# Layer 0's down projection by Strassen's scheme, in a two-layer decoder kernel

## The chip, the cores and the metric

The kernel runs on one core of a Trainium2 chip. The metric is the device time of one execution in microseconds (us). Engines are called PE (TensorE, matmuls), DVE (VectorE), ACT (ScalarE), POOL (GpSimd) and SP (SyncE, which issues most DMAs).

## The reference

Two layers on 512 tokens of width 1024, all in fp32. Layer 0 is a Mamba-2 mixer and a ConvFFN; then keys and values are projected from the normed stream; layer 1 is differential attention and a ConvFFN. The change lies in layer 0's ConvFFN, in its last matrix product:

```python
def conv_ffn(x, ln_g, up_w, conv_w, conv_b, down_w):
    u = causal_dwconv(rms_norm(x, ln_g) @ up_w, conv_w, conv_b)
    gate, up = u[..., :FFN_DIM], u[..., FFN_DIM:]
    return (jax.nn.silu(gate) * up) @ down_w          # FFN_DIM = 2816

def shared_kv(x, kv_ln_g, kv_w, k_norm_g):            # on the stream behind layer 0
    kv = rms_norm(x, kv_ln_g) @ kv_w
    ...
```

## The kernel before, in words

The stream is held transposed, as `xT`: eight blocks of 128 features by 512 tokens. Each fp32 value is split into a high half that fits PE's fast fp32 form and the rest, so a product takes three matmuls: high by high, high by low, low by high (`mm3`, L208 to L210). For the stream the halves are `xgh` (ACT, L483) and `xgl` (DVE, L484).

Weights come in chunks of at most 128x1024, in the order of a list, `plan`. For each chunk SP loads the raw tile `wr`, ACT copies the high half `wh` (L148, `high`), DVE subtracts for the low half `wl` (L159, `low`). Taking a chunk emits the work on the chunks up to two places ahead of it (`chunk`, `emit_chunk`). The chunks for keys and queries are scaled by a gain as they are split (L173 on ACT, L174 on DVE). PSUM has two rings of four banks, `mm` and `aux`.

A ConvFFN is the function `ffn`. Its 22 hidden blocks of 128 features run in parts: gate and up products of a part first ("g" and "u" chunks), then the part's share of the down projection. A gate or up product has 24 matmuls of 512 columns; its taps are an addition-like step on DVE (L957), one on ACT (L958) and two of 511 or 510 elements on DVE (L960); then come SiLU (ACT, L1127) and the product of both (DVE).

Layer 0 has two parts, of 12 and 10 blocks. Each hidden block is split into `hh` (L1140, ACT) and `hl` (L1141, DVE), 512 tokens wide. The down projection takes four groups of 256 features (two banks `ps_d` each); weights are stationary, tokens move, 512 columns a matmul. After each group `add_to_stream` adds both banks to `xT` (L571). In the last part it also makes `xgh` and `xgl` for the next projection, squares the block (L557, ACT) and adds the square to the norm's sum `nacc` (L559, on POOL, for the last block on DVE).

Layer 1 already uses Strassen's scheme (`down_tokens`) in parts of 8, 8 and 6 blocks. There a pair of hidden blocks (even and odd) and two token halves give four quarters; `operands` builds four sums of them (L1035) and splits them (`sh` L1038 ACT, `sl` L1039 DVE). The weights' sums are made by accumulating DMAs that POOL issues into the tiles `wz` (`plus`, L986) or by DVE; `combine` splits them (L1008, L1009). The seven products are named "1" to "7", in the order 1257634; a running sum of some of them collects what several outputs share (L1059). In layer 1 the token operands are stationary and 512 weight columns move.

Behind layer 0's FFN the first projection is `k0` (function `proj`), whose chunks of two feature blocks are read in the order 0, 2, 4, 6. The Tile framework's scheduler orders each engine's queue; waits between engines are semaphores. PE's queue is written by hand in attention alone.

Of the kernel before, what the change touches and what calls it, by code (L numbers as in the profile page):

```python
# [18 lines left out]
P = 128  # L19
T = 512  # L20
# [12 lines left out]
SEVEN = "1257634"  # L33
# [8 lines left out]
def trunk_kernel(ctx: ExitStack, tc, x, ssm_ln_g, ssm_in_w, ssm_conv_w, ssm_conv_b, ssm_dt_bias,  # L42
# [48 lines left out]
    def ffn_plan(l):  # L91
        for p0, p1 in PARTS_D if l else ((0, HALF), (HALF, NPAIR)):
            for p in range(p0, p1):
                plan.append(("g%d_%d" % (l, p), *w_cols(ffn_up_w[l], 0, KB, p * P, P)))
                plan.append(("u%d_%d" % (l, p), *w_cols(ffn_up_w[l], 0, KB, FFN + p * P, P)))
            if l == 1:
                for m in SEVEN:
                    for q0 in range(0, (p1 - p0) // 2, 2):
                        plan.append(("s%s_%d_%d" % (m, p0, q0), (m, p0, q0, min(2, (p1 - p0) // 2 - q0))))
                continue  # L100
            for c in range(4):
                for k in range(p0, p1, 4):
                    plan.append(("d%d_%d_%d" % (l, c, k),
                                 *w_cols(ffn_down_w[l], k, min(4, p1 - k), c * 256, 256)))

    ffn_plan(0)

    def tok_plan(key, w, c0, gcol):
        for k in range(0, KB, 2):
            plan.append(("%s_%d" % (key, k), *w_cols(w, k, 2, c0, 512), gcol + k))  # L110
# [78 lines left out]
    def emit_chunk():  # L189
        i = state["next"]  # L190
        if i < len(plan):
            state["next"] = i + 1
            if len(plan[i]) == 2:
                state["combine"](plan[i][0], *plan[i][1])
# [39 lines left out]
    xgh = [gp.tile([P, T], F32R, name="xgh%d" % k) for k in range(KB)]  # L234
    xgl = [gp.tile([P, T], F32R, name="xgl%d" % k) for k in range(KB)]
# [265 lines left out]

    def token_rsqrt(acc, pl, name, n):
# [42 lines left out]
    class Norm:  # L545
# [6 lines left out]
        def add(self, k):  # L552
# [6 lines left out]
            (dve if k == KB - 1 else pool).tensor_tensor(out=self.acc, in0=self.acc, in1=sq, op=ALU.add)  # L559

# [373 lines left out]
    def ffn(l, norm, bp, gnext, nnext):  # L934
        with tc.tile_pool(name="ffn_h%d" % l, bufs=1) as hp, tc.tile_pool(name="ffn%d" % l, bufs=1) as fp:
# [13 lines left out]
            def taps(j, p, ps):  # L949
# [4 lines left out]
                v = fp.tile([P, T], F32, tag="v%d" % j, name="v" + key, bufs=3 if j or nnext is not None else 4)  # L954
# [21 lines left out]
            raws = {}  # L976

            def source(p0, q0, nq, j, i):
                src = ffn_down_w[l][(p0 + 2 * q0) * P:(p0 + 2 * q0 + 2 * nq) * P, i * 512:(i + 1) * 512]
                return src.rearrange("(k j p) c -> j p k c", j=2, p=P)[j]  # L980

            def view(t, nq):
                return t[:, :nq * 512].rearrange("p (k c) -> p k c", k=nq)

            def plus(t, p0, q0, nq, j, i):
                pool.dma_start(view(t, nq), source(p0, q0, nq, j, i), accum_op=ALU.add)  # L986

            def ahead(p0, n, behind):

                for k, j, i in ("z", 0, 0), ("x", 0, 1), ("y", 1, 1):  # L990
                    for q0 in range(0, n // 2, 2):
                        c, nq = q0 // 2, min(2, n // 2 - q0)
                        pool.tensor_copy(raws[k][c][:, 0:1], behind[:, 0:1])
                        sync.dma_start(view(raws[k][c], nq), source(p0, q0, nq, j, i))

            def combine(key, m, p0, q0, nq):

                c, n = q0 // 2, nq * 512
                if m == "2":
                    t = wrp.tile([P, 1024], F32, tag="raw", name="wr_" + key)  # L1000
                    sync.dma_start(view(t, nq), source(p0, q0, nq, 1, 0))
                else:
                    t = raws["x" if m == "7" else "y" if m == "3" else "z"][c]
                    if m == "7":
                        dve.tensor_tensor(out=t[:, :n], in0=t[:, :n], in1=raws["y"][c][:, :n], op=ALU.add)
# [5 lines left out]
                if m in "156":  # L1011
                    plus(t, p0, q0, nq, *{"1": (0, 1), "5": (1, 1), "6": (1, 0)}[m])

            if nnext is None:
                raws["z"] = [fp.tile([P, 1024], F32, name="wz%d" % c) for c in range(2)]
# [3 lines left out]
                state["combine"] = combine  # L1019
                run_sum = fp.tile([P, 2, T], F32, name="run_sum")  # L1020

            def operands(p, ga, sides):

                h = ga.rearrange("p (i t) -> p i t", i=2)
                if p % 2 == 0:
                    sh = hp.tile([P, 7, 256], F32R, tag="sh", name="sh%d" % p, bufs=4)
                    sl = hp.tile([P, 7, 256], F32R, tag="sl", name="sl%d" % p, bufs=4)
                    sides.append((sh, sl, h))
                    parts = [(slice(0, 1), h[:, 0:1, :])]
                else:  # L1030
                    sh, sl, e = sides[-1]
                    s = fp.tile([P, 4, 256], F32, tag="sums", name="sums%d" % p, bufs=1)
                    for o, a, b, op in ((0, e[:, 1], h[:, 1], ALU.subtract), (1, s[:, 0], e[:, 0], ALU.subtract),
                                        (2, e[:, 0], e[:, 1], ALU.subtract), (3, h[:, 0], s[:, 1], ALU.add)):
                        dve.tensor_tensor(out=s[:, o], in0=a, in1=b, op=op)  # L1035
                    parts = [(slice(3, 7), s), (slice(1, 3), h)]
# [4 lines left out]
            def down_tokens(p0, n, sides, last):  # L1041
# [30 lines left out]
                for m in SEVEN:  # L1072
# [3 lines left out]
                    for q0 in range(0, nq, 2):  # L1076
                        wh, wl = chunk("s%s_%d_%d" % (m, p0, q0))
# [41 lines left out]
            for p0, p1 in PARTS_D if nnext is None else ((0, HALF), (HALF, NPAIR)):  # L1119
                last = p1 == NPAIR  # L1120
                hh, hl, sides = [], [], []
                for p in range(p0, p1):
# [8 lines left out]
                    if nnext is None:  # L1131
                        dve.tensor_tensor(out=ga, in0=ga, in1=up, op=ALU.mult)
                        operands(p, ga, sides)
                        if p == p0 + 2:
                            ahead(p0, p1 - p0, ga)
                        continue
                    h = hp.tile([P, T], F32R, tag="hh", name="hh%d_%d" % (l, p), bufs=HALF + 1)
                    w = hp.tile([P, T], F32R, tag="hl", name="hl%d_%d" % (l, p), bufs=HALF + 1)
                    dve.tensor_tensor(out=ga, in0=ga, in1=up, op=ALU.mult)
                    act.activation(h, ga, AF.Copy)  # L1140
                    dve.tensor_tensor(out=w, in0=ga, in1=h.bitcast(F32), op=ALU.subtract)  # L1141
                    hh.append(h)
                    hl.append(w)
                n = p1 - p0
                if nnext is None:
                    down_tokens(p0, n, sides, last)
                    continue
                for c in range(4):
# [380 lines left out]
```

## Time and profile before

| | |
|---|---|
| median of 3 runs | 1334.04 us (1333.04 to 1334.26) |
| profiled execution | 1333.75 us, its span 1332.1 us |
| mean granted TensorE clock | 0.999 of full speed |
| busy: PE, DVE, ACT, POOL | 1325.3, 1001.3, 671.6, 121.8 us |
| layer 0's down stages | 508.0 to 573.4 and 682.2 to 736.5 us of the span |
| layer 1's down stages | 1067.8 to 1105.9, 1193.0 to 1231.0, from 1296.3 us |

The page gives busy time by engine, a row of 40 slices, the DMA queues, the chain of waits that ended last and the costliest groups of instructions. A timeline row has the start, the time to the end of the last of its instructions, the engine and line, output and inputs, shapes and the count, and in brackets the idle time before it and what ended that. Durations of successive instructions overlap somewhat, so the time that one takes in a stream is read from start to start.

### The profile page before, as it was taken

What the parts mean: (1) busy time and instruction counts of PE and PEld (TensorE: products, weight loads), DVE (VectorE), ACT (ScalarE), POOL (GpSimd) and SP (SyncE); (2) the same over time, 40 slices, a digit from 0 to 9 for tenths busy, and PEclk for the clock granted to TensorE, in tenths of its full rate; (3) what the DMA queues carried; (4) which work ended last, traced back from release to release, by engine and by line L of the source; (5) the groups of instructions that cost most, each with busy time, mean ns of one, the idle gap of its engine ahead of it and who ended that gap; (6) DMA issues with size and microseconds to landing.
All of it is one profiled execution on the core that took longest, in us unless ns stands there. A gap on an engine that the chain in (4) does not pass through costs nothing.

```text
span 1332.1 us, 17130 instructions
## 1 busy us (share of the span) xinstructions
PE 1325.3 (99%) x6399; PEld 1088.0 (82%) x6399; DVE 1001.3 (75%) x1678; ACT 671.6 (50%) x1104; POOL 121.8 (9%) x175
## 2 busy tenths in 40 slices
PE   9999999999999999999999999999999999999998
PEld 8878888888888888888888887777788888888886
DVE  7989888789877775357764646777778987888788
ACT  6696554752444442134443556777654443454443
POOL 5230300200110000000001200000020010001001
PEclk9999999999999999999999999999999999999999
DMA  7553533432333333333323422222126353544444
GB/s 207 159 154 96 148 98 111 135 95 72 95 95 95 95 95 95 96 100 103 98 86 93 130 84 84 75 76 56 57 87 190 95 111 103 184 109 81 125 135 111
DMA packets 184371, 143.65 MB, mean 108 GB/s; under 512 B 6812, under 2 KB 163872, under 8 KB 184288
## 3 DMA queue, kind: packets, MB, share of 16 engines
q1 hardware_dynamic: 173904, 120.73, 30.5%
q0 software_dynamic: 9104, 20.73, 7.0%
q8 instruction: 50, 0.82, 0.3%
q10 hardware_dynamic: 1280, 1.10, 0.2%
q14 instruction: 33, 0.27, 0.1%
HBM read 140.29 MB, written 2.25 MB: 107 GB/s over the span
## 4 chain that ended last, share of the span: by engine, by line
PE 94%; DVE 4%; ACT 1%; DMA 1%; issue 0%; SPq 0%; POOL 0%; DVEq 0%; ACTq 0%
PE ps_g L209 5%; PE ps_u L208 5%; PE ps_g L210 5%; PE ps_g L208 5%; PE ps_u L209 5%; PE ps_u L210 5%; PE ps_in L208 5%; PE ps_in L210 5%; PE ps_in L209 5%; PE ps_d L210 3%; PE ps_d L209 3%; PE ps_d L208 3%; PE ps_s L1056 2%; PE ps_s L1055 2%; PE ps_s L1053 2%; PE ps_o L209 2%
## 5 line engine op out<-in xcount | busy, mean ns | idle before, releaser
L208 PE MATMUL ps_u<-xgh,wh_u 128*128 128x512 f32 x352 | 137.4, 390 | 0.0
L209 PE MATMUL ps_g<-xgl,wh_g 128*128 128x512 f32 x352 | 137.1, 389 | 0.0
L208 PE MATMUL ps_g<-xgh,wh_g 128*128 128x512 f32 x352 | 137.0, 389 | 0.0
L210 PE MATMUL ps_u<-xgh,wl_u 128*128 128x512 f32 x352 | 137.0, 389 | 0.0
L210 PE MATMUL ps_g<-xgh,wl_g 128*128 128x512 f32 x352 | 137.0, 389 | 0.0
L209 PE MATMUL ps_u<-xgl,wh_u 128*128 128x512 f32 x352 | 136.9, 389 | 0.0
L208 PE MATMUL ps_in<-xgh,wh_in 128*128 128x512 f32 x304 | 122.9, 404 | 0.0
L210 PE MATMUL ps_in<-xgh,wl_in 128*128 128x512 f32 x304 | 119.7, 394 | 0.0
L209 PE MATMUL ps_in<-xgl,wh_in 128*128 128x512 f32 x304 | 119.2, 392 | 0.0
L209 PEld LDWEIGHTS ps_g<-xgl,wh_g 128*128 128x128 f32 x352 | 66.1, 188 | 13.9 <-DVE xgl L488 0.3
L210 PEld LDWEIGHTS ps_u<-xgh,wl_u 128*128 128x128 f32 x352 | 66.1, 188 | 13.8
L957 DVE TENSOR_TENSOR uu<-ps_u,nr_f 128x512 f32<-128x512 f32 x44 | 30.4, 691 | 62.5 <-PE ps_u L210 62.5
L208 PEld LDWEIGHTS ps_g<-xgh,wh_g 128*128 128x128 f32 x352 | 66.1, 188 | 13.7
L210 PEld LDWEIGHTS ps_g<-xgh,wl_g 128*128 128x128 f32 x352 | 66.0, 188 | 13.7
L209 PEld LDWEIGHTS ps_u<-xgl,wh_u 128*128 128x128 f32 x352 | 66.1, 188 | 13.6
L208 PEld LDWEIGHTS ps_u<-xgh,wh_u 128*128 128x128 f32 x352 | 66.0, 188 | 13.5
L1127 ACT ACTIVATE vg<-vg 128x512 f32<-128x512 f32 x44 | 27.8, 633 | 84.0 <-DVE vg L960 84.0
L148 ACT ACTIVATE wh_u<-wr_u 128x1024 fp32r<-128x1024 f32 x44 | 46.8, 1063 | 43.8 <-PE ps_g L209 35.4
L208 PE MATMUL ps_d<-hh,wh_d 128*128 128x512 f32 x176 | 68.5, 389 | 0.0
L209 PE MATMUL ps_d<-hl,wh_d 128*128 128x512 f32 x176 | 68.5, 389 | 0.0
L210 PE MATMUL ps_d<-hh,wl_d 128*128 128x512 f32 x176 | 68.5, 389 | 0.0
L960 DVE SCALAR_TENSOR_TENSOR vu<-uu,cf,vu 128x511 f32<-128x511 f32 x88 | 65.8, 748 | 3.1 <-ACT vu L958 1.7
(394 smaller groups left out, 3246.2 us busy)
## 6 DMA issues: line engine op xcount, KB each, us to landing
wr_g<-in_ffn_up_w_dram SPq DMA_DIRECT2D x44, 512.0 KB, 3.8
wr_u<-in_ffn_up_w_dram SPq DMA_DIRECT2D x44, 512.0 KB, 3.9
wr_in<-in_ssm_in_w_dram SPq DMA_DIRECT2D x40, 512.0 KB, 3.9
wr_d<-in_ffn_down_w_dram SPq DMA_DIRECT2D x20, 512.0 KB, 3.5
m<-cumd POOLq DMA_DIRECT2D x16, 512.0 KB, 4.9
wr_out<-in_ssm_out_w_dram SPq DMA_DIRECT2D x16, 512.0 KB, 3.5
wz<-in_ffn_down_w_dram POOLq DMA_DIRECT2D x15, 512.0 KB, 6.0
xT<-in_ffn_down_w_dram SPq DMA_DIRECT2D x10, 512.0 KB, 7.0
```

Of the source, the lines that this page charges most:

```text
L148: return act.activation(self.wh[:, :self.n], self.raw[:, :self.n], AF.Copy)
L208: pe.matmul(ps, wh, xh, start=start, stop=False)
L209: pe.matmul(ps, wh, xl, start=False, stop=False)
L210: return pe.matmul(ps, wl, xh, start=False, stop=stop).ins
L957: dve.tensor_tensor(out=u, in0=ps, in1=r, op=ALU.mult)
L960: dve.scalar_tensor_tensor(out=v[:, s:], in0=u[:, :T - s], scalar=col(2 - s), in1=v[:, s:], op0=ALU.mult, op1=ALU.add)
L1053: pe.matmul(pss[b], h, ws[q][1][:, cols], start=False, stop=end and q == qs[-1])
L1055: pe.matmul(pss[b], h, ws[q][0][:, cols], start=first and q == qs[0], stop=False)
L1056: pe.matmul(pss[b], w, ws[q][0][:, cols], start=False, stop=False)
L1127: act.activation(ga, ga, AF.Silu)
```

## The change

Layer 0's down projection runs by the same scheme, in a form of its own (`down_features`): weights stay stationary and a quarter of the tokens' operand moves, 256 columns a matmul. Layer 0 now has three parts, of 8, 8 and 6 blocks. The seven products come in the order 5126743, each for two groups `c` of 512 output features (two blocks of the first column half, two of the second). For every product and `c` there is one chunk of weights, of 1024 elements in the first two parts and 768 in the last. Both 128-feature blocks of a product share a bank. Each product is added to the quarter or quarters of `xT` that contain it; products 1, 6 and 7 go through `run_sum`.

For a pair of blocks with token halves e0, e1 (even block) and h0, h1 (odd), the operands are e0 ("1"), h0 ("2"), h1 ("3"), s0 = e1-e0 ("5"), s1 = h1-s0 ("6"), e1-h1 ("7") and h0-s1 ("4"). The weights' sums need additions alone, all of them by accumulating DMAs: tile `wz` starts as W01+W11 ("5"), then gets W00 ("6") and W10 ("3"); tile `wx` starts as W00 ("1") and gets W01 ("7"); "2" and "4" are plain loads.

In the last part a quarter of two blocks (512 elements) that is complete is split and squared at once: `scaled_part` and `add_part`. Squares collect in two tiles, `nsum0` and `nsum1`, one for each token half; POOL adds five of them, DVE the last, and two additions of 256 elements on DVE close `nacc`. The projection `k0` reads its chunks in the order 2, 6, 0, 4. `xgh` and `xgl` are now one tile each.

```diff
-SEVEN = "1257634"
+SEVEN = "5126743", "1257634"
 ...
-        for p0, p1 in PARTS_D if l else ((0, HALF), (HALF, NPAIR)):
+        for p0, p1 in PARTS_D:
 ...
+            for m in SEVEN[l]:
+                for c in range(0, nq, 2) if l else range(2):
+                    plan.append(("s%d%s_%d_%d" % (l, m, p0, c), (l, m, p0, c, min(2, nq - c) if l else nq)))
+    def tok_order(key):
+        return (2, 6, 0, 4) if key == "k0" else range(0, KB, 2)
 ...
+    def scaled_part(k, h):
+        v, hi, lo = (t[:, k:k + 2, h * 256:(h + 1) * 256] for t in (xTt, xght, xglt))
+        act.activation(hi, v, AF.Copy)
+        dve.tensor_tensor(out=lo, in0=v, in1=hi.bitcast(F32), op=ALU.subtract)
 ...
+        def add_part(self, k, h):
+            self.seen = getattr(self, "seen", [])
+            v = xTt[:, k:k + 2, h * 256:(h + 1) * 256]
+            self.seen.append(h)
+            n = len(self.seen)
+            s = self.sums[h]
+            if self.seen.count(h) == 1:
+                act.activation(s, v, AF.Square)
+                return
+            sq = self.pl.tile([P, T], F32, tag="nsq", name="nsq_%s%d_%d" % (self.name, k, h), bufs=2)
+            sq = sq.rearrange("p (a t) -> p a t", a=2)
+            act.activation(sq, v, AF.Square)
+            (dve if n == KB else pool).tensor_tensor(out=s, in0=s, in1=sq, op=ALU.add)
+            if self.seen.count(h) == 4:
+                dve.tensor_tensor(out=self.acc[:, h * 256:(h + 1) * 256], in0=s[:, 0], in1=s[:, 1], op=ALU.add)
 ...
+                for k, j, i in (("z", 0, 0), ("x", 0, 1), ("y", 1, 1)) if l else (("x", 0, 0), ("z", 0, 1)):
 ...
+                        if k == "z" and not l:
+                            plus(t, p0, c, nq, 1, 1)
 ...
+                more = ({"1": (0, 1), "5": (1, 1), "6": (1, 0)} if l else {"1": (0, 1), "5": (0, 0), "6": (1, 0)}).get(m)
+                if more:
+                    plus(t, p0, c, nq, *more)
 ...
                 if p % 2 == 0:
 ...
+                    if not l:
+                        sums = [(0, h[:, 1], h[:, 0], sub)]
+                        parts.append((slice(3, 4), s[:, 0:1]))
 ...
+                        sums = [(1, h[:, 1], s[:, 0], sub), (2, e[:, 1], h[:, 1], sub), (3, h[:, 0], s[:, 1], sub)]
+                        parts = [(slice(1, 3), h), (slice(4, 7), s[:, 1:4])]
 ...
+            def down_features(p0, n, sides, last):
 ...
+                for m in SEVEN[0]:
+                    for c in range(2):
+                        wh, wl = chunk("s0%s_%d_%d" % (m, p0, c))
+                        ps = (aux_bank if m in "274" else mm_bank)("ps_s%s_%d_%d" % (m, p0, c))
+                        v = halves(ps)
+                        for b in range(2):
+                            for low in range(2):
+                                for q in range(nq):
+                                    h, w = (t[:, side[m], :] for t in sides[q][:2])
+                                    cols = slice(b * P, (b + 1) * P)
+                                    if low:
+                                        pe.matmul(v[:, b], wl[:, q, cols], h, start=False, stop=q == nq - 1)
+                                        continue
+                                    pe.matmul(v[:, b], wh[:, q, cols], h, start=q == 0, stop=False)
+                                    pe.matmul(v[:, b], wh[:, q, cols], w, start=False, stop=False)
+                        rs_ = run_sum[:, c, :]
+                        r = halves(rs_)
+                        if m == "5":
+                            add(c, 0, 1, v, ALU.subtract)
+                            add(c, 1, 1, v)
+                        elif m == "1":
+                            add(c, 0, 0, v)
+                            act.activation(rs_, ps, AF.Copy, scale=-1.0)
+                        elif m == "2":
+                            add(c, 0, 0, v)
+                            ended(c, 0, 0)
+                        elif m == "6":
+                            dve.tensor_tensor(out=rs_, in0=rs_, in1=ps, op=ALU.add)
+                            add(c, 0, 1, r, ALU.subtract)
+                        elif m == "7":
+                            dve.tensor_tensor(out=rs_, in0=rs_, in1=ps, op=ALU.add)
+                            add(c, 1, 1, r)
+                            ended(c, 1, 1)
+                            add(c, 1, 0, r)
+                        elif m == "4":
+                            add(c, 1, 0, v)
+                            ended(c, 1, 0)
+                        else:
+                            add(c, 0, 1, v)
+                            ended(c, 0, 1)
 ...
-                for c in range(4):
-                    pss = [mm_bank("ps_d%d_%d_%d" % (l, p0, 2 * c + i)) for i in range(2)]
-                    for k0 in range(0, n, 4):
-                        wh, wl = chunk("d%d_%d_%d" % (l, c, p0 + k0))
-                        for i in range(2):
-                            for k in range(k0, min(n, k0 + 4)):
-                                mm3(pss[i], wh[:, k - k0, i * P:(i + 1) * P],
-                                    wl[:, k - k0, i * P:(i + 1) * P], hh[k], hl[k], k == 0, k == n - 1)
-                    for i in range(2):
-                        m = 2 * c + i
-                        add_to_stream(m, pss[i], gnext, nnext if last else None)
```

How the change moves instructions shows at two places. The first is PE's queue where layer 0's first down stage begins; a row has the line, the operation, output and inputs with their numbers, and the shape. Before, behind the twelfth "u" product:

```order
L210 MATMUL ps_u0_11_4625<-xgh7_93,wl_u0_11_4542 128x512
L208 MATMUL ps_d0_0_0_4661<-hh0_0_3776,wh_d0_0_0_4583 128x512
L209 MATMUL ps_d0_0_0_4661<-hl0_0_3777,wh_d0_0_0_4583 128x512
L210 MATMUL ps_d0_0_0_4661<-hh0_0_3776,wl_d0_0_0_4584 128x512
L208 MATMUL ps_d0_0_0_4661<-hh0_1_3856,wh_d0_0_0_4583 128x512
L209 MATMUL ps_d0_0_0_4661<-hl0_1_3857,wh_d0_0_0_4583 128x512
```

The same place in the changed kernel, behind the eighth "u" product (`ps_s5_0_0` is product "5" of the part from block 0, group 0; `sh0` and `sl0` hold the quarters of blocks 0 and 1):

```order
L208 MATMUL ps_u0_7_4331<-xgh_86,wl_u0_7_4245 128x512
L1188 MATMUL ps_s5_0_0_4375<-sh0_3770,wh_s05_0_0_4289 128x256
L1189 MATMUL ps_s5_0_0_4375<-sl0_3771,wh_s05_0_0_4289 128x256
L1188 MATMUL ps_s5_0_0_4375<-sh2_3937,wh_s05_0_0_4289 128x256
L1189 MATMUL ps_s5_0_0_4375<-sl2_3938,wh_s05_0_0_4289 128x256
L1188 MATMUL ps_s5_0_0_4375<-sh4_4114,wh_s05_0_0_4289 128x256
L1189 MATMUL ps_s5_0_0_4375<-sl4_4115,wh_s05_0_0_4289 128x256
L1188 MATMUL ps_s5_0_0_4375<-sh6_4281,wh_s05_0_0_4289 128x256
L1189 MATMUL ps_s5_0_0_4375<-sl6_4282,wh_s05_0_0_4289 128x256
L1186 MATMUL ps_s5_0_0_4375<-sh0_3770,wl_s05_0_0_4290 128x256
```

A product runs over pairs of blocks, and the matmuls that need the weights' low half (L1186) now stand together behind the others.

The second place is DVE's queue at the end of the FFN, where the k0 projection begins. Before:

```order
L159 TENSOR_TENSOR wl_d0_3_16_6084<-wr_d0_3_16_6081,wh_d0_3_16_6083 128x1024
L571 TENSOR_TENSOR xT_85<-ps_d0_12_4_6019,xT_85 128x512
L571 TENSOR_TENSOR xT_85<-ps_d0_12_5_6020,xT_85 128x512
L159 TENSOR_TENSOR wl_d0_3_20_6116<-wr_d0_3_20_6113,wh_d0_3_20_6115 128x512
L484 TENSOR_TENSOR xgl4_98<-xT_85,xgh4_90 128x512
L484 TENSOR_TENSOR xgl5_99<-xT_85,xgh5_91 128x512
L174 SCALAR_TENSOR_TENSOR wl_k0_0_6146<-wr_k0_0_6143,c2_103,wh_k0_0_6145 128x512 x2
L174 SCALAR_TENSOR_TENSOR wl_k0_2_6178<-wr_k0_2_6175,c2_103,wh_k0_2_6177 128x512 x2
L571 TENSOR_TENSOR xT_85<-ps_d0_12_6_6111,xT_85 128x512
L571 TENSOR_TENSOR xT_85<-ps_d0_12_7_6112,xT_85 128x512
```

In the changed kernel:

```order
L1036 TENSOR_TENSOR wl_s03_16_0_6726<-wz0_0_3659,wh_s03_16_0_6725 128x768
L503 TENSOR_TENSOR xgl_87<-xT_85,xgh_86 128x2x256
L1168 TENSOR_TENSOR xT_85<-xT_85,ps_s4_16_0_6729 128x2x256
L1036 TENSOR_TENSOR wl_s03_16_1_6755<-wz0_1_3660,wh_s03_16_1_6754 128x768
L1168 TENSOR_TENSOR xT_85<-xT_85,ps_s4_16_1_6758 128x2x256
L503 TENSOR_TENSOR xgl_87<-xT_85,xgh_86 128x2x256
L172 SCALAR_TENSOR_TENSOR wl_k0_2_6787<-wr_k0_2_6784,c2_89,wh_k0_2_6786 128x512
L503 TENSOR_TENSOR xgl_87<-xT_85,xgh_86 128x2x256
L579 TENSOR_TENSOR nacc_kv_3652<-nsum0_3663 128x256
L172 SCALAR_TENSOR_TENSOR wl_k0_2_6787<-wr_k0_2_6784,c2_89,wh_k0_2_6786 128x512
L1168 TENSOR_TENSOR xT_85<-xT_85,ps_s3_16_0_6792 128x2x256
```

Before, both pairs of k0's first scaled weights stand ahead of the stream's last additions; now the first of them stands behind the last down weights (`wl_s03_16_1`), an addition and a quarter's split, and the norm sum's closing addition (`nacc_kv`) stands between the two halves of one chunk.

More of the change, by code (lines that the diff above doesn't have):

```diff
@@ L193, in emit_chunk @@
             if len(plan[i]) == 2:
[L194 removed]
+                state["combine"](plan[i][0], *plan[i][1][1:])
                 return
@@ L233, in trunk_kernel @@
     xT = [xTt[:, k, :] for k in range(KB)]
-    xgh = [gp.tile([P, T], F32R, name="xgh%d" % k) for k in range(KB)]
-    xgl = [gp.tile([P, T], F32R, name="xgl%d" % k) for k in range(KB)]
+    xght, xglt = (gp.tile([P, KB, T], F32R, name=n) for n in ("xgh", "xgl"))
+    xgh, xgl = ([t[:, k, :] for k in range(KB)] for t in (xght, xglt))
     c1 = cp.tile([P, P], F32, name="c1")
@@ L985, in plus @@
-            def plus(t, p0, q0, nq, j, i):
-                pool.dma_start(view(t, nq), source(p0, q0, nq, j, i), accum_op=ALU.add)
+                return t[:, :nq * ncol].rearrange("p (k c) -> p k c", k=nq)
+            def plus(t, p0, c, nq, j, i):
+                pool.dma_start(view(t, nq), source(p0, c, nq, j, i), accum_op=ALU.add)
             def ahead(p0, n, behind):
[L990 to L994, printed above, removed]
@@ L1122, in ffn @@
+            for p0, p1 in PARTS_D:
+                sides = []
                 for p in range(p0, p1):
@@ L1190, in proj @@
             pss = [mm_bank("ps_%s_%d" % (key, b)) for b in range(NT)]
-            for k0 in range(0, KB, 2):
+            order = tok_order(key)
+            for k0 in order:
                 wh, wl = chunk("%s_%d" % (key, k0))
@@ L1202, in proj @@
                     if b % 2:
-                        if k0 == 0 and b == 3:
+                        if k0 == order[1] and b == 1:
                             if not rts:
@@ L1207, in proj @@
                                 rts.append(norm_kv.col())
-                        if k0 + 2 == KB:
+                        if k0 == order[-1]:
                             for i in (b - 1, b):
```

111 lines of the change are left out of this document (56 added, 55 removed).

## The prediction

> **What bounds the kernel now.** The page's first part and the list of PE's waits come first.
>
> ```profile
> PE 1325.3 (99%) x6399; PEld 1088.0 (82%) x6399; DVE 1001.3 (75%) x1678; ACT 671.6 (50%) x1104; POOL 121.8 (9%) x175
> PE warm L292 <- DVE ones L219: 1.1, 1, 1.1
> ```
>
> PE is busy for 1325.3 of the span's 1332.1 us, and only its first wait, 1.1 us, is put down to a semaphore. So a matmul taken out shortens the run, as long as the work that feeds PE keeps up. The windows say how close it is. Their columns are start and end in us, the five engines' busy time and, behind them, TensorE's clock, the DMA share and GB/s.
>
> ```profile
> 508.00:573.40 65.40, 65.40 (x290) 54.17 (x289) 23.04 (x24) 14.19 (x15) 0.00 (x0) 1.00 0.33 97
> 573.40:682.20 108.80, 108.80 (x482) 90.09 (x481) 76.84 (x96) 47.74 (x59) 0.00 (x0) 1.00 0.31 95
> 682.20:736.50 54.30, 54.30 (x242) 44.95 (x241) 26.25 (x32) 19.17 (x29) 7.43 (x5) 1.00 0.31 92
> 1067.80:1105.90 38.10, 38.10 (x169) 31.53 (x168) 33.19 (x43) 18.71 (x20) 4.83 (x4) 1.00 0.51 96
> 1193.00:1231.00 38.00, 38.00 (x169) 31.48 (x168) 33.15 (x43) 18.61 (x20) 4.83 (x4) 1.00 0.50 95
> 1296.30:1332.00 35.70, 30.40 (x130) 23.34 (x128) 30.21 (x46) 13.60 (x18) 4.19 (x4) 0.96 0.50 111
> ```
>
> Rows one and three are layer 0's two down stages: PE full, DVE 23.04 of 65.40 and 26.25 of 54.30. Row two is the ten up pairs between them, with DVE at 71%. Rows four and five are layer 1's first two down parts, already by Strassen's scheme: DVE is at 33.2 of 38.1, 87%, and PE never waits. The last row is layer 1's last part and the kernel's end.
>
> **The matmuls.** The present products, and the nearest 256-column ones (in the mixer's input projection), each row with the row that follows it where a spacing is read:
>
> ```profile
> L208 PE MATMUL ps_d<-hh,wh_d x176: 389/389/389, 508.0 to 735.8; 128*128 128x512 f32 x176
> L208 PEld LDWEIGHTS ps_d<-hh,wh_d x176: 187/188/188, 507.8 to 735.6; 128*128 128x128 f32 x176
> 19.22 1.12 PE L339 MATMUL ps_in<-xgh,wl_in 128*128 128x256 f32 x8
> 20.17 0.40 PE L452 MATMUL ps_in<-xgh,wh_in 128*128 128x512 f32 x1
> ```
>
> Three such groups of 176 are 528 matmuls. They fill windows one and three, 119.7 us, without a gap: 0.2267 us each. Durations overlap, so I count starts: eight 256-column matmuls from 19.22 to 20.17 are 0.119 us each, 0.525 of the wide one. The changed kernel runs seven products for each of 11 block pairs, two column groups c, two row blocks b and three precision terms: 7x11x2x2x3 = 924 at 256 columns. 924x0.119 = 110.0, so PE's own work falls by **9.7 us** (8.8 if a narrow one takes 0.120).
>
> A rule of the Trainium skill speaks against this term. "TensorE: Matmul & The Clock Gate", section "Back-to-back issue gap", gives sustained spacings of about 81 ns at 128 columns and 131 ns at 512, so half the columns are far from half the time. An estimate on the straight line between them is 98 ns at 256, 0.746 of the wide one; scaled to this stage 924x0.746x0.2267 = 156 us, 37 more than now. The trace's 0.525 disagrees, and the sum goes by the trace.
>
> **The up stages.** An operand is no longer one split of 512 elements but seven quarters for two blocks. DVE's durations, again from start to start:
>
> ```profile
> 1301.71 0.68 DVE L1132 TENSOR_TENSOR vg<-vg,vu 128x512 f32<-128x512 f32 x1
> 1302.32 0.68 DVE L1059 TENSOR_TENSOR xr<-xr,ps_s 128x512 f32<-128x512 f32 x1
> 1302.91 0.42 DVE L1035 TENSOR_TENSOR sums<-vg,vg 128x256 f32<-128x256 f32 x1
> 1303.25 0.68 DVE L1039 TENSOR_TENSOR sl<-vg,sh 128x512 fp32r<-128x512 f32 x1
> 1308.68 1.82 DVE L1009 TENSOR_TENSOR wl_s<-xT,wh_s 128x1024 fp32r<-128x1024 f32 x2
> 1310.42 2.47 DVE L1059 TENSOR_TENSOR xr<-xr,ps_s 128x512 f32<-128x512 f32 x4
> ```
>
> An instruction of 256 elements takes 0.34 us, of 512 0.60, and the pair of 1024 and 512 takes 1.74, so 1024 takes 1.14; 768 I put between, at 0.87. For two blocks the two old subtractions (1.20) become four sums (1.36) and subtractions of 256, 256, 512 and 768 (2.15): 1.15 us more per block. Window two's 76.84 over ten blocks is 7.7 each; 8.9 of PE's 10.9 remains covered. Products "5" and "1" open a part and use the even blocks' quarters alone, so the last odd block's chain has 4x24x0.119 = 11.4 us before product "2" needs it. I cost the up stages at **nothing**; if the chain were late, once per part, by 1 us, that would be 3.
>
> **Down parts one and two.** With four pairs PE needs 14x24x0.119 = 40.0 us. DVE has 14 weight subtractions of 1024 (16.0), 22 additions of 512 to the residual stream xT and to the running sum (13.2), and the last odd block.
>
> ```profile
> 510.19 1.53 DVE L960 SCALAR_TENSOR_TENSOR vu<-uu,cf,vu 128x511 f32<-128x511 f32 x2
> 511.75 0.69 DVE L1139 TENSOR_TENSOR vg<-vg,vu 128x512 f32<-128x512 f32 x1
> ```
>
> That block's taps are an instruction of 512 and these two (0.60+1.56), then come the product (0.60), three sums (1.0) and subtractions of 512 and 768 (1.47): 5.2. In all 34.4, or 86%. Layer 1 at that share shows no wait. **Nothing**, with 0 to 2 us each as the bound.
>
> **The last part**, with three pairs, is where I expect a loss. PE needs 14x18x0.119 = 30.0 us. Behind the last "u" product DVE's queue holds, in its order up to the last weights' low half: 12 subtractions of 768 (10.4), 19 additions (11.4), four quarter subtractions xgl (2.4) and operands and taps (5.2), 29.4 us. Two more costs lie on it. One is waiting for accumulating DMAs:
>
> ```profile
> 1305.94 2.12 POOL L986 DMA_DIRECT2D wz<-in_ffn_down_w_dram  x2 [10.23 <-DVE sums L1035]
> 1312.40 1.06 ACT L1008 ACTIVATE wh_s<-wz 128x1024 fp32r<-128x1024 f32 x1 [4.55 <-DMA wz<-in_ffn_down_w_dram]
> ```
>
> In layer 1's last part ACT waits 4.55 us for such a landing, and DVE behind it 0.6. I take 1.0, between them. The other is POOL's additions for the norm:
>
> ```profile
> 710.66 2.38 DVE L484 TENSOR_TENSOR xgl<-xT,xgh 128x512 fp32r<-128x512 f32 x2
> 711.04 3.15 POOL L559 TENSOR_TENSOR nacc_kv<-nacc_kv,nsq_kv 128x512 f32<-128x512 f32 x2 [11.28 <-ACT nsq_kv L557]
> 697.06 0.68 DVE L484 TENSOR_TENSOR xgl<-xT,xgh 128x512 fp32r<-128x512 f32 x1
> ```
>
> Two of the subtractions beside two POOL additions last 2.38 us, where alone they would take 0.60+0.68: 0.55 us lost per addition. Two of the five POOL additions fall ahead of the last weights: 1.1. The Trainium skill's "SBUF — State Buffer", section "SBUF: two separate sides", lets a DVE instruction with two SBUF inputs and a POOL one that reads SBUF shut each other out for the whole instruction. By that rule an addition could cost DVE up to its own 1.6 us here, some 2 us more in all; the row shows only a third of that.
>
> So the last low half is ready at about 29.4+1.0+1.1 = 31.5, and six low matmuls (0.7) follow: 32.2, **2 us** behind PE's 30.0. Then the k0 projection, now begun with blocks 2 and 3, needs more from the same queue: an addition, a quarter subtraction, the scaled weights of block 2, another subtraction, the norm sum's half (it waits for POOL) and the weights of block 3.
>
> ```profile
> 734.52 1.42 DVE L174 SCALAR_TENSOR_TENSOR wl_k<-wr_k,c,wh_k 128x512 fp32r<-128x512 f32 x2 [4.03 <-ACT wh_k L173]
> 735.85 1.50 DVE L571 TENSOR_TENSOR xT<-ps_d,xT 128x512 f32<-128x512 f32 x2
> ```
>
> Two scaled ones take 1.33 to the next start, 0.67 each. That is 3x0.60+0.34+2x0.67 = 3.5 us, and about 1 more for POOL; before block 3's weights PE has the six low matmuls and block 2's three, 1.4 us. The hand-over costs about **3 us**, where now it costs none. From below, a DVE that keeps up gives 0 for both terms together; from above, dearer waits for the DMAs (7.8 us is the longest landing) and the full lock give 9. I take 5.
>
> ```profile
> DMA to landing us min/median/max: 3.8/5.9/7.8
> ```
>
> **The sum.** The profiled run took 1333.75 us (span 1332.1 and 1.65 around it), 0.29 under the median of the runs, 1334.04; I sum against the first. 1333.75 - 9.7 + 0 + 0 + 2 + 3 = **1329.0** (rounded). Attention, layer 1's FFN and all ahead of layer 0's FFN keep their order, so they add nothing.
>
> **The rivals.** A difference of 0.2%, 2.7 us, is about what a measurement of this kernel can tell from no change.
>
> A. *DVE keeps up*: the waits fall into PE's own slack, 0 to 2 us in place of 5: 1324 to 1326. For it: in the last window DVE is as full (30.21 us), and yet the 130 matmuls kept PE busy for 30.40, hardly more than the 29.5 that they make at 0.2267. Against: that part has no norm behind it. Chance 0.15.
>
> B. *The gain is eaten*: at 87% the first two parts stall too, 2 us each, because additions meet weights late on one queue. 1329+4 = 1333, no change that could be told. For it: 22 additions a part where the old stages had eight. Against: layer 1's windows. Chance 0.13.
>
> C. *Narrow matmuls are dearer over a long stream*: the change pays only while 924 of them plus the 5 lost stay under 119.7, so up to 0.124 us each; above 0.127 it is slower by over 0.2%. At 0.130 the time is 1333.75-119.7+120.1+5 = 1339. For it: a part's stream is 336 matmuls long, and the quoted one eight. Against: those eight. Chance 0.08.
>
> D. *The weight load sets the pace*: each narrow matmul brings a load of its own, recorded at 188 ns. If loads did not overlap one another, 924x0.188 = 174 and the time is 1333.75-119.7+174+5 = 1393. Against: the eight keep 0.119 with just such loads. Chance 0.02. The skill's spacings, above, make a milder case of the same kind: by its ratio the time is 1375.
>
> E. *The scheme is not there*: the program's order shows 924 such matmuls and no 512-column ones in their place. Chance 0.
>
> **How the numbers follow.** The forecast, 1329.0, has the remaining 0.62; its own range is 1326 to 1331.3. The range 1324.0 to 1333.5 takes in A and most of B and leaves out C, D and the edges, less than 0.2. Faster by over 0.2%: forecast and A, 0.77; within 0.2%: B, 0.13; slower: C and D, 0.10.
>
> **What would show it.** In the changed kernel's profile: products ps_s of 256 columns 0.119 us from start to start; first and second down stage 40.0 us each with PE full; in the last one PE idle for DVE's low halves and xgl, some 5 us up to k0's second block; up pairs still 10.9 us of PE; layer 1 as now. I am wrong if a narrow matmul takes over 0.122, if PE idles within the first two parts, or if the hand-over to k0 shows under 2 or over 8 us of idle time.

## The result, and the profile after

The changed kernel takes 1337.72 us (median of 14 runs, 1335.19 to 1341.39) against 1333.63 us (14 runs, 1332.87 to 1335.2): a ratio of 1.003, with a 95% interval of 1.0022 to 1.0039. It is slower by 4 us, and its runs spread 6.2 us, against 2.3. The forecast was 1329.0, and the time lies above its range.

The profiled execution is one of the quickest of the fourteen: 1335.32 us, span 1333.4, clock 1.000. Its page and PE's list of waits (place, what released it, us in total, times, longest):

```profile
PE 1318.6 (99%) x6795; PEld 1100.3 (83%) x6795; DVE 1074.8 (81%) x1814; ACT 700.5 (53%) x1150; POOL 153.1 (11%) x210
PE ps_q L1271 <- ACT knk L1293: 3.2, 1, 3.2
PE ps_k L1272 <- DVE wl_k L172: 2.7, 2, 1.7
PE ps_s L1186 <- DVE wl_s L1036: 1.6, 2, 0.9
```

PE works 6.7 us less than before, but waits in three new places. The second and third were forecast. The first, the longest, lies in q0, a projection that the change does not touch. The windows of the down parts, of k0 and of q0 show how much each stage cost:

```profile
464.80:505.20 40.40, 40.40 (x338) 40.36 (x338) 34.42 (x44) 18.23 (x20) 5.06 (x4) 1.00 0.64 129
592.20:632.50 40.30, 40.30 (x337) 40.28 (x336) 34.44 (x44) 18.13 (x20) 5.08 (x4) 1.00 0.64 130
697.80:730.20 32.40, 30.77 (x254) 30.33 (x253) 32.13 (x47) 21.55 (x32) 8.93 (x7) 1.00 0.58 117
730.20:755.70 25.50, 22.82 (x102) 18.33 (x101) 15.84 (x31) 11.60 (x18) 9.31 (x25) 1.00 0.37 106
755.70:783.60 27.90, 24.34 (x114) 19.45 (x113) 14.94 (x26) 14.48 (x25) 0.00 (x0) 1.00 0.39 120
```

The first two down parts run as forecast: PE full for 40.3 us, DVE at 34.4. In the last two rows, windows in which PE was never idle before the change, it is idle for 2.7 and 3.6 us. Where each stage starts in the two traces (the first matmul on its tile):

| first matmul of | before | after | gained (-) or lost (+) in the stage ahead of it |
|---|---|---|---|
| layer 0's FFN (ps_g) | 376.5 | 376.9 | +0.4 |
| k0 (ps_k) | 736.5 | 730.2 | -6.7, the FFN |
| q0 (ps_q) | 758.7 | 755.7 | +3.3, k0 |
| v0 (ps_v) | 782.3 | 783.6 | +4.3, q0 |
| end of the span | 1332.1 | 1333.4 | 0.0, all the rest |

At q0's first matmul the change is 3.0 us ahead; in q0 it loses 4.3. The chain of waits, in the stretch that ends with PE's wait, shows with what (start, us, what):

```profile
740.95 0.34 DVE nacc_kv L579
741.29 0.67 DVE wl_k L172
742.05 4.42 DMA rb<-in_rel_bias_dram
746.52 3.13 POOL bv L1255 x18
749.65 0.36 POOL bd L1256
750.16 1.66 DMA bd<-bv
752.06 3.84 DMA tr<-bd
755.92 0.44 DVE tb L1340
756.38 3.04 DMA tr<-bd
759.44 0.43 DVE tb L1340
759.87 0.60 DVE ssk L1295
760.55 0.63 ACT ksqk L1294
761.18 0.58 ACT knk L1293
761.81 0.50 PE ps_q L1271
```

This is layer 1's table of position biases. POOL loads `rel_bias`, spreads it into `bv` and stores it to DRAM as `bd`; SP loads it back as `tr`, and DVE copies that into `tb`. Nobody needs `tb` before attention, but its two copies stand on DVE ahead of k0's row sums `ssk`. ACT empties k0's next bank only when the sums have freed its scratch tile, and PE, which has done q0's first two blocks of tokens by then, has no bank for the third. The same three rows of DVE's timeline before the change, and POOL's row that starts the chain, before and after:

```profile
750.29 0.43 DVE L1266 COPY tb<-tr 128x512 f32<-128x512 f32 x1 [5.07 <-DMA tr<-bd]
753.75 0.43 DVE L1266 COPY tb<-tr 128x512 f32<-128x512 f32 x1
756.19 0.69 DVE L1221 TENSOR_REDUCE ssk<-ksqk 128x8 f32<-128x512 f32 x1 [0.57 <-ACT ksqk L1220]
736.92 0.74 POOL L1172 DMA_DIRECT2D rb<-in_rel_bias_dram  x1 [9.13 <-PE ps_d L210]
```

```profile
742.05 0.78 POOL L1245 DMA_DIRECT2D rb<-in_rel_bias_dram  x1 [4.18 <-DVE wl_k L172]
```

Before, the second copy was done 2 us ahead of the first row sum. The load of `rb` goes into memory that the FFN's tiles held, so it waits for their last reader. That was a down matmul of PE; now the sums of squares `nsum0` and `nsum1` lie there too, and their last reader on DVE is the norm's closing addition (`nacc_kv`, done at 741.3). The row itself names `wl_k`, the instruction behind that addition on DVE (done at 742.0); that the load waits for the addition is read from the program, and the experiments test it. The chain starts 5.1 us later, while k0 starts 6.3 us earlier.

### The profile page after: what moved, and what is told of

It is laid out like the page before. It is cut to its first block, busy times and chain, and to the rows that moved or that the text cites. A ratio compares the mean times of both kernels' runs of the same rounds, so it can differ in the third digit from the quotient of the medians.

```text
span 1333.4 us, 18218 instructions
## 1 busy us (share of the span) xinstructions
PE 1318.6 (99%) x6795; PEld 1100.3 (83%) x6795; DVE 1074.8 (81%) x1814; ACT 700.5 (53%) x1150; POOL 153.1 (11%) x210
## 4 chain that ended last, share of the span: by engine, by line
PE 89%; DVE 6%; DMA 2%; ACT 1%; issue 1%; POOL 0%; SPq 0%; DVEq 0%; ACTq 0%
PE ps_g L207 5%; PE ps_u L207 5%; PE ps_u L206 5%; PE ps_g L208 5%; PE ps_g L206 5%; PE ps_u L208 5%; PE ps_in L206 5%; PE ps_in L208 5%; PE ps_in L207 5%; PE ps_s L1188 2%; PE ps_s L1189 2%; PE ps_s L1186 2%; PE ps_s L1094 2%; PE ps_o L207 2%; PE ps_o L206 2%; PE ps_o L208 2%
## 5 line engine op out<-in xcount | busy, mean ns | idle before, releaser
L1189 PE MATMUL ps_s<-sl,wh_s 128*128 128x256 f32 x308 | 77.4, 283 | 0.0
L1188 PE MATMUL ps_s<-sh,wh_s 128*128 128x256 f32 x308 | 77.4, 283 | 0.0
L1008 POOL DMA_DIRECT2D wz<-in_ffn_down_w_dram x36 | 43.7, 1255 | 290.3 <-DVE wl_s L1036 224.2
L1079 ACT ACTIVATE sh<-vg 128x256 fp32r<-128x256 f32 (+1 forms) x44 | 23.0, 524 | 98.2 <-DVE vg L1227 98.1
```

The lines of the kernel that those rows point to most:

```text
L1008: pool.dma_start(view(t, nq), source(p0, c, nq, j, i), accum_op=ALU.add)
L1079: act.activation(sh[:, o], v, AF.Copy)
L1188: pe.matmul(v[:, b], wh[:, q, cols], h, start=q == 0, stop=False)
L1189: pe.matmul(v[:, b], wh[:, q, cols], w, start=False, stop=False)
```

## The experiments

The theory: PE's own gain is as forecast, and the table's late start turns it into a wait in q0. Two rivals: k0's evacuation is late by itself, since the norm closes later in the projection; or the narrow matmuls and the last part cost more than one trace shows. A second question was the spread, 1335 to 1341 us.

**The changed kernel again**, unchanged.

> The changed kernel once more, unchanged, for a second trace and for its clock. All theories: about 1337.7 us against 1333.6. In the first trace (1335.3 us, clock 1.000) PE loses 4.3 us in one new place, behind the k0 projection, where it waits 3.2 us for ACT's evacuation of k0. Theory of the clock: the 14 runs spread from 1335.2 to 1341.4 with their granted clock from 1.000 down to 0.995, so the rest (2.4 us at the median) is clock; a trace at 0.998 or less then shows a stretch with a granted clock below 1.00 that the first trace does not have, and it stands next to a gap on PE. Rival: the spread has nothing to do with the clock, and a slow trace shows longer waits instead.

Measured: 1336.68 us (1335.93 to 1338.97), ratio 1.0025 (1.0015 to 1.0035). Its trace has a clock of 0.998 and waits longer in q0. PE's timeline there, and two windows of which the third column from the end is the clock:

```profile
757.67 0.39 PE L1273 MATMUL ps_q<-wh_q,xgl 128*128 128x512 f32 x1
762.44 0.79 PE L1271 MATMUL ps_q<-wh_q,xgh 128*128 128x512 f32 x1 [4.39 <-ACT knk L1293]
763.04 0.63 PE L1272 MATMUL ps_q<-wl_q,xgh 128*128 128x512 f32 x1
...
765.60 0.43 PE L1272 MATMUL ps_q<-wl_q,xgh 128*128 128x512 f32 x1
765.87 0.40 PE L1273 MATMUL ps_q<-wh_q,xgl 128*128 128x512 f32 x1
```

```profile
755.00:760.00 5.00, 3.06 (x14) 2.20 (x12) 1.75 (x3) 0.00 (x0) 0.00 (x0) 1.00 0.43 137
760.00:765.00 5.00, 2.56 (x6) 2.07 (x7) 2.92 (x5) 3.58 (x7) 0.00 (x0) 0.73 0.44 140
```

Behind the gap seven matmuls take 3.2 us from start to start, 0.43 each and more for the first, where they take 1.6 at full clock. The first trace had no such stretch behind its 3.2 us gap. So both theories of the spread hold in part: the gap itself varies (3.2 and 4.4 us), and in some runs a stretch at half the clock adds 1.6 us. The Trainium skill's "TensorE: Matmul & The Clock Gate", section "What's actually happening", says that the gate halves the clock after an idle window of about 3.4 us and that these windows run freely. These two traces agree: one program, in one run with and in one without the slow stretch of 3.2 us.

**The table early.**

```diff
+    ep = ctx.enter_context(tc.tile_pool(name="table", bufs=1, side="right"))
+    rb = ep.tile([AH, 32], F32, name="rb")
+    bd = dp.tile([AH, NBIAS], F32, name="bd")
+    pool.dma_start(rb, rel_bias.rearrange("b h -> h b"))
...
     norm_kv = Norm(bp, "kv")
     ffn(0, norm, bp, None, norm_kv)
...
-        rb = ap.tile([AH, 32], F32, name="rb")
-        bd = dp.tile([AH, NBIAS], F32, name="bd")
-        pool.dma_start(rb, rel_bias.rearrange("b h -> h b"))
...
```

> The changed kernel with the bias table of layer 1 (POOL's load of rel_bias, its copies and the two stores to DRAM) made ahead of layer 0's FFN, from tiles of a small pool of its own. Theory: DVE's queue holds the copies of that table (tb) ahead of k0's row sums, and they wait for a chain that begins only when the FFN's memory is released, which the norm sums nsum now put off; with the table early the 3.2 us wait of ps_q goes and the time falls by about 4.3 us, to 1331 from a trace's 1335.3; if the clock falls because of that gap it also returns to 0.999 in all runs, so the median falls by some 6.5, to 1331, 2.5 below the kernel before. Rival: k0's evacuation is late by itself, since its norm is closed later in the projection; then PE still waits 3 us or more there and the time stays at 1336 to 1338.

Measured: 1331.97 us (1330.93 to 1332.3), ratio 0.9987 (0.9978 to 0.9996). The wait in q0 is gone from the list, and DVE's copies come 5 us ahead of the sums:

```profile
746.49 0.43 DVE L1341 COPY tb<-tr 128x512 f32<-128x512 f32 x1 [0.77 <-DMA tr<-bd]
749.95 0.43 DVE L1341 COPY tb<-tr 128x512 f32<-128x512 f32 x1 [0.25 <-DMA tr<-bd]
755.20 0.69 DVE L1296 TENSOR_REDUCE ssk<-ksqk 128x8 f32<-128x512 f32 x1 [0.58 <-ACT ksqk L1295]
```

Against the changed kernel on the same chip that is 4.7 us less. It is enough to turn the change from slower to slightly faster. The rival, an evacuation of k0 that is late by itself, falls with this run. Its eleven executions spread 1.4 us with a clock of 0.998 or 0.999, where the eight of the changed kernel as it was, on the same chip, spread 3.0 us with a clock down to 0.995: most of the spread went with the gap. The time is still 3 us above the forecast, and this trace has the slow clock at the hand-over to k0, behind waits of 0.97 and 1.73 us:

```profile
730.00:735.00 5.00, 2.30 (x13) 1.50 (x12) 5.00 (x6) 2.73 (x5) 3.07 (x2) 0.94 0.00 2
735.00:740.00 5.00, 5.00 (x17) 3.97 (x18) 5.00 (x8) 2.30 (x4) 1.82 (x1) 0.72 0.64 189
```

So no single gap as long as the Trainium skill's window was needed: PE was busy for 2.30 of 5 us there. Nor do these two gaps always bring it: the first trace has 0.96 and 1.72 us at the same place, and its clock stays at 1.00.

**The table early in the kernel before**, the same edit.

> The kernel before with the table made ahead of layer 0's FFN, as in table_early, and nothing else changed. Theory: before the change the table's copies on DVE stood ahead of k0's row sums too, but came in time (750.3 and 753.8 us; the sums began at 756.2), so making them earlier brings nothing: 1333.5 to 1334.2. Rival: the early table is a gain of its own, 2 to 5 us, which has nothing to do with the changed FFN: 1329 to 1332.

Measured: 1334.16 us (1333.43 to 1336.34), ratio 1.0005 (0.9997 to 1.0014). The early table is no gain of its own.

**The table late in the kernel before.** The last square goes into a tile of the FFN's pool, so the release waits for DVE's last addition; in a second run the table also makes one more trip through DRAM.

```diff
+            if k == KB - 1 and self.last_sq is not None:
+                sq = self.last_sq
+            else:
+                sq = self.pl.tile([P, T], F32, tag="nsq", name="nsq_%s%d" % (self.name, k), bufs=2)
...
+            if nnext is not None:
+                nnext.last_sq = fp.tile([P, T], F32, name="lastsq")
```
```diff
-            pool.dma_start(bd[:, i * hb:(i + 1) * hb], bv)
+            pool.dma_start(bd0[:, i * hb:(i + 1) * hb], bv)
+        pool.dma_start(bd, bd0)
```

> The kernel before, with nothing of Strassen's scheme in layer 0, but with the square of the last stream block kept in a tile of the FFN's pool, so that the memory's release, and with it the bias table, waits for the norm's last addition on DVE (240 in place of 236.4 or so on the trace's scale of 700 us). Theory: the table's copies on DVE come some 4 us later and hold k0's row sums, PE waits 1 to 3.5 us in q0, and the time is 1335 to 1338, with a clock that spreads as in the changed kernel. Rival: the release has no part in it: 1333.6, no wait in q0.

> The kernel before, with the table's release put off as in the run before_late and the finished table sent through one more copy in DRAM, so that it is some 3 us later still. No Strassen product in layer 0. In before_late the table's copies on DVE fell to 755.6 and 759.3 us and the time rose by 0.7 us. Theory of the table: k0's row sums now wait until about 762 to 763, PE waits 3 to 4 us in q0, and the time is 1337 to 1339. Theory of the clock: a gap of over 3 us on PE can be followed by some 3.4 us of matmuls at half the clock (0.43 us for 0.227), so the runs spread over about 2 us and their clock goes from 0.999 down to 0.996. Rival: the changed kernel's loss in q0 needs its own late norm; then 1334 to 1335, clock 0.999.

Measured: 1334.34 us (1333.42 to 1336.3, and one run of 2708.86), ratio 1.0006 (0.9997 to 1.0015), for the first, no change that can be told; 1336.17 us (1335.44 to 1340.93), ratio 1.0024 (1.0015 to 1.0033), for the second. DVE's timeline of the first, and the wait that the second alone has:

```profile
759.34 0.43 DVE L1272 COPY tb<-tr 128x512 f32<-128x512 f32 x1 [2.03 <-DMA tr<-bd]
759.68 0.68 DVE L1227 TENSOR_REDUCE ssk<-ksqk 128x8 f32<-128x512 f32 x1
```

```profile
PE ps_q L1205 <- ACT knk L1227: 1.6, 1, 1.6
```

In the first the load of `rb` starts at 741.6 us in place of 736.9, with a `wl_k` behind the norm's last addition named as its releaser, as in the changed kernel: a tile with a late reader in that memory is enough for it. The sums come 3.5 us later, about as in the changed kernel (3.7), but k0 ends at 758.7 here and not at 755.7, so most of that is covered. The second makes the wait and a loss of 2.3 us in a kernel without a Strassen product in layer 0. Both times were below the expected ones, which I put down to the longer cover behind k0. Its clock stayed at 0.999 or 1.000 in ten of eleven runs, where I had expected it to fall to 0.996: that half of the expectation is a miss.

**Strassen's scheme in two parts alone**, the third part plain, with the norm and k0's order of the kernel before.

```diff
+            if l == 0 and p1 == NPAIR:
+                for c in range(4):
+                    for k in range(p0, p1, 4):
+                        plan.append(("d%d_%d_%d" % (l, c, k),
+                                     *w_cols(ffn_down_w[l], k, min(4, p1 - k), c * 256, 256)))
+                continue
...
-        return (2, 6, 0, 4) if key == "k0" else range(0, KB, 2)
+        return range(0, KB, 2)
...
+                    if plain:
...
+                        act.activation(h, ga, AF.Copy)
+                        dve.tensor_tensor(out=w, in0=ga, in1=h.bitcast(F32), op=ALU.subtract)
...
+                            add_to_stream(2 * c + i, pss[i], gnext, nnext)
```

> The changed kernel with Strassen's scheme in layer 0's first two parts alone; the third part (six blocks) is done by eight plain products of 512 columns, with the norm sums, the order of k0 and the splits of the kernel before. Theory: 672 narrow matmuls of 0.120 us replace 384 of 0.2267, 87.1 - 80.6 = 6.4 us less; the first two parts show no wait, the hand-over to k0 costs nothing, and the table is as early as before: 1333.6 - 6.4 = about 1327, clock 0.999. Rival (the gain is lost in the first two parts or in the up stages as well): 1330 or more, with waits there.

Measured: 1327.59 us (1326.51 to 1327.94), ratio 0.9955 (0.9942 to 0.9967). That is 6.1 us less for 6.4 expected, with no wait in the FFN or behind it. This kernel has no `nsum` tiles, and in its trace the load of `rb` waits for a down matmul of PE again and starts at 731.6 us. The price of a narrow matmul, the up stages and the first two parts are settled by this run; what is lost lies at the last part.

**The last part's loss**, three runs from the kernel with the table early (1331.97). First POOL's additions of squares moved to DVE, then k0's natural order:

```diff
-            (dve if n == KB else pool).tensor_tensor(out=s, in0=s, in1=sq, op=ALU.add)
+            dve.tensor_tensor(out=s, in0=s, in1=sq, op=ALU.add)
```
```diff
-        return (2, 6, 0, 4) if key == "k0" else range(0, KB, 2)
+        return range(0, KB, 2)
```

> The changed kernel with the table early (1332.0 us) and the norm's five additions of squares, done by POOL, on DVE instead. In the trace DVE's subtractions beside two POOL additions at the hand-over to k0 took 1.77 us each where alone they take 0.74 and 0.68. Theory: POOL's additions are 2.1 us of the 2.7 us that PE waits for k0's weights; on DVE they cost 1.2 there, so the wait falls to about 1.8, and with gaps that short the clock stays up (in table_early seven matmuls behind the gap took 0.43 us, 1.4 us in all): 1329.5 to 1331. Rival: DVE is full anyway and five additions more (3.0 us) make it later: 1333 or more.

> The changed kernel with the table early (1332.0 us) and k0's chunks in the order 0, 2, 4, 6 as before the change. Blocks 0 and 1 get their last quarter from product 3, the last, so k0's second token half waits for an addition, a split on ACT and one on DVE behind the last product. Theory: PE waits 1 to 3 us more at the hand-over: 1333 to 1335. Rival: the hand-over is bound by DVE's queue whatever the order: 1332.

Measured: 1332.06 us (1330.92 to 1333.25) and 1331.61 us (1331.21 to 1334.18); neither differs from 1331.97. With the additions on DVE the wait for k0's weights fell from 2.7 to 1.9 us, as expected, but the other waits grew and nothing was won: a missed expectation. The order of k0 brings nothing either: I had expected a loss of 1 to 3 us, and its rival, a hand-over bound by DVE's queue whatever the order, fits. What both leave alone is that DVE reaches the end of the part late. The third run gives it time there, by parts of 6, 8 and 8 blocks:

```diff
-PARTS_D = (0, 8), (8, 16), (16, 22)
+PARTS_D = ((0, 6), (6, 14), (14, 22)), ((0, 8), (8, 16), (16, 22))
-        for p0, p1 in PARTS_D:
+        for p0, p1 in PARTS_D[l]:
```

> The changed kernel with the table early (1332.0 us) and layer 0's parts of 6, 8 and 8 blocks in place of 8, 8 and 6. Theory: the loss in the last part is DVE's queue against PE's 30 us; with four pairs PE has 40 us there for DVE's 33, so the 1.6 us of waits for the low halves go, and the hand-over shrinks since DVE is less behind; the first part, now with three pairs but no norm, loses under 1 us: 1329 to 1331. Rival: the loss is in the hand-over's own chain and stays, 1331 to 1333, or the first part stalls by more than 1.5 us.

Measured: 1325.21 us (1324.73 to 1325.88), ratio 0.9937 (0.9924 to 0.9949), 8.6 us less than before and quicker than I expected. PE's list of waits has nothing left of the FFN, of k0 or of q0 but this row:

```profile
PE ps_g L207 <- DVE xgl L486: 0.3, 1, 0.3
```

**The same parts with the table late.**

> The changed kernel with layer 0's parts of 6, 8 and 8 blocks, but with the table late again, as in the change. With the table early these parts gave 1325.2 us. Theory: the table's chain still begins behind the norm's last addition, k0 ends as long behind it as in the changed kernel or sooner, and PE waits 4 us or more in q0: 1329 to 1332, with a spread of 2 us or more. Rival: with DVE less behind, the norm closes early enough and the table does no harm: 1325 to 1326.

Measured: 1329.64 us (1328.68 to 1331.22), ratio 0.9969 (0.9958 to 0.9979), with one wait of that length in q0, shorter than the 4 us expected:

```profile
PE ps_q L1271 <- ACT knk L1293: 2.5, 1, 2.5
```

Behind it eight matmuls start 0.43 us apart, and the clock is 0.66 from 755 to 760 us: a single gap of 2.5 us was enough here. The late table costs 4.4 us in these parts (1329.64 against 1325.21, on two chips whose kernels before differ by 0.1), 4.7 in the change's own, and an early one brings nothing in the kernel before. The theory of the table stands, by undoing it and with other parts. In the old kernel the late release alone was covered, and only with a table that was later still did the wait show.

## Why the prediction was wrong

**The matmuls**: right, at the lower of the two gains that were given. PE's timeline of the changed kernel, where a part begins:

```profile
464.84 0.28 PE L1188 MATMUL ps_s<-sh,wh_s 128*128 128x256 f32 x1
466.27 0.28 PE L1188 MATMUL ps_s<-sh,wh_s 128*128 128x256 f32 x1
467.71 0.28 PE L1188 MATMUL ps_s<-sh,wh_s 128*128 128x256 f32 x1
```

Twelve matmuls lie between each two of these rows: 0.120 each for 0.119, so 924 of them save 8.8 us. Rivals C and D fall with it, and with them the spacings of the Trainium skill's "TensorE: Matmul & The Clock Gate", section "Back-to-back issue gap", which this trace contradicts over streams of 336.

**The up stages and the first two parts**: right, no wait in either. Rival B falls. The time of rival A, 1324 to 1326, was reached only with the table early and other parts.

**The last part and the hand-over**: 2 + 3 forecast, 1.6 of waits in the part and 3.3 lost in k0 measured. The sum was right, but partly by luck: three of its pieces were wrong and about cancel. The 1.0 us for accumulating DMAs was not paid at all: from 698 us to the end of the part neither DVE nor ACT waits for a DMA. Behind the last low half PE had twelve matmuls left (728.7 to 730.2 us), not six, since the second block's high products come behind the first block's low ones; that is 0.7 us more in the part, and 0.7 less in the hand-over, which they cover. And POOL's additions were dearer at the hand-over. Inside the part one lengthens a weight subtraction by 0.5 us, as reckoned (two such rows, and POOL's addition beside the second); at the hand-over it is twice that (the last three rows):

```profile
725.08 0.95 DVE L1036 TENSOR_TENSOR wl_s<-wz,wh_s 128x768 fp32r<-128x768 f32 x1
727.15 1.46 DVE L1036 TENSOR_TENSOR wl_s<-wz,wh_s 128x768 fp32r<-128x768 f32 x1
726.09 1.70 POOL L577 TENSOR_TENSOR nsum<-nsum,nsq_kv 128x512 f32<-128x512 f32 x1 [9.49 <-ACT nsq_kv L576]
729.73 1.77 DVE L172 SCALAR_TENSOR_TENSOR wl_k<-wr_k,c,wh_k 128x512 fp32r<-128x512 f32 x1
731.42 1.77 DVE L503 TENSOR_TENSOR xgl<-xT,xgh 128x512 fp32r<-128x512 f32 x1
729.34 3.30 POOL L577 TENSOR_TENSOR nsum<-nsum,nsq_kv 128x512 f32<-128x512 f32 x2 [1.55 <-ACT nsq_kv L576]
```

Each of DVE's two instructions at the hand-over lost some 1.1 us, twice the 0.55 that I had taken from the old trace. That lies between my reading and the rule of the Trainium skill's "SBUF — State Buffer", section "SBUF: two separate sides", by which the loser waits for the whole instruction (1.65 us here).

**The step that failed** is the sentence behind the sum: "Attention, layer 1's FFN and all ahead of layer 0's FFN keep their order, so they add nothing." The projections between the FFN and attention are not even named in it, and the sum has no term for them behind the hand-over. The order on each queue was kept there, but not the times. The table's chain hangs on the release of the FFN's memory, the change put a tile with a late reader into that memory, and DVE's queue carries the wait to k0's row sums. That is 4.3 us in the first trace, more than the 3.0 that were won by then. From the forecast to this trace it is 6.3 us: these 4.3, 0.9 for the dearer matmuls, and 1.1 in small pieces elsewhere. No rival had it: rival B put the loss into the first two parts. In the old trace the row of `rb` waiting for `ps_d` and that of `tb` waiting 5.07 us for `tr` were both there to be read; the second copy had 2 us to spare.

The rest of the loss, from the first trace's 1.6 us above before to the median's 4.1, is spread over the runs: their clock goes from 1.000 to 0.995, and the second trace shows half a clock behind a gap. That gaps set it off is seen in four traces with such a stretch inside the kernel (the changed kernel again, the table early, k0's natural order, and the parts of 6, 8 and 8 with the table late) and none without a gap ahead of it; it was not tested by itself, and no trace was kept of a run at 0.995, so what happens in the slowest runs stays open.

## What to carry to other kernels

A tile that is added to a pool delays whatever takes over that pool's memory, until the tile's last reader is done; look up who that is and what waits for the first load behind it. A step that nobody needs yet is not free if its wait stands at the head of an in-order queue: move such preparation well ahead, or behind the work that is needed. Where a stage's engine is nearly full, give the longest part to the end, where its results are handed over: parts of 6, 8 and 8 with the table early brought nearly all of the 8.8 us that the saved matmuls are worth.

## What the runs showed of the hardware that was not expected

- A gap on PE can cost more than its length: behind gaps of 4.4 us, of 2.5 us, or of 0.97 and 1.73 us with little work between, matmuls of 512 columns took 0.43 us for 0.227 over 3.1 to 3.4 us, some 1.5 us lost. The changed kernel also ran without that, behind a gap of 3.2 us.
- DVE and POOL slow each other: at the hand-over by 1.1 us for an instruction of DVE, and POOL's own addition took 1.65 us, where the quickest in the trace before took 1.29.
- With 256 columns the weight loads' records fill PEld's whole stage (40.36 of 40.40 us, at 192 ns each), and yet a matmul starts every 0.120 us.
